# Attention bias loaded whole per head instead of formed on GpSimd, and gate rows summed one step later in the merge

## The chip, the cores and the metric

The kernel runs on one core of a Trainium2 chip. Its engines are TensorE (PE; its weight loads are listed apart as PEld), VectorE (DVE), ScalarE (ACT), GpSimd (POOL) and SyncE (SP), which here only issues DMA transfers; ACT and POOL issue some as well. Each engine works through its own instruction queue in order, and the engines meet through semaphores. The metric is the device time of one execution in microseconds, lower is better. Times are compared by the median of several executions.

## The reference, cut to what matters

One layer runs on 128 context tokens and 512 latent tokens (a grid of 8 rows by 64 columns) of width 1024. It has a Hyena branch and an attention branch on the same modulated input; they are gated, projected, merged and normalised. The change touches the bias of the neighbourhood attention and the gate of the merge:

```python
s_win = einsum("brqhd,brkhd->bhrqk", qg, kg) * scale
in_win = (key_col[None, :] >= c0[:, None]) & (key_col[None, :] < c0[:, None] + kw)
bias = rpb[:, dr + WIN_ROWS_MAX - 1, clip(dc + WIN_COLS - 1, 0, 2 * WIN_COLS - 2)]
s_win = where(in_win[None, None, None], s_win + bias[None], NEG_INF)
s_ctx = einsum("brqhd,bkhd->bhrqk", qg, ctx_k) * scale
p = softmax(concatenate([s_win, s_ctx], axis=-1), axis=-1)
...
p_h = (y_h * silu(g_h)) @ w_bh
p_a = (y_a * silu(g_a)) @ w_ba
out = (sigmoid(m_h) * p_h + sigmoid(m_a) * p_a) @ w_out
...
shift, scale, gate = split(silu(cond) @ w_ada + b_ada, 3)
x_new = layer_norm(ALPHA * x + gate * out)
```

There are 16 heads of width 64. The bias depends on the head and on the offset between query and key, the mask on the columns alone.

## The kernel before

**Precision.** Nearly every product is made of three passes of fp32r matmuls: both operands are split into a high and a low part. `split` (L100 to L102) makes the high part with a copy on ACT and the low part with a subtraction on DVE. A weight tile of 128 by 1024 is loaded into a `raw` buffer (two of them, `wraw`, L131), split into `wh` (two buffers) and `wl` (three buffers, `wtile`, L135) and used by 48 matmuls of 320 columns (`proj`, L173: 8 k-steps, 3 passes, 2 halves of the 640 tokens; one half to each of two PSUM banks). There are four PSUM banks of the kind `mm`, so two projections can be open at once.

**Order.** The program is traced in one order and then put in order for each engine by a planner that works with a simulated time. Only instructions in a `manual_schedule` block (the prologue on three engines; PE alone during attention) and those pinned by `keep_in_program_order` (behind the instruction traced before on the same engine) are placed by hand. `load_to` (L62) issues a load on SP and pins it while `pinned[0]` holds; that is so in the prologue and again from L1162, the merge, and not in attention.

**Attention (about 380 to 712 us).** For each pair of heads j = 0 to 7 there are four blocks b of 128 queries. `attention_setup` (L781) loads the mask, clears three strips of four `tm` tiles on POOL and forms the first two heads' tiles. `bias_tile` (L803) forms a head's bias tile `tm` (128 by 1024, negated, with the mask's fill): one load of 128 KB on SP into `tb` and three subtractions on POOL (L807, L810, L811), pinned from the third head on. `block_probs` (L878) asks for the next pair's two tiles at b = 1. `probs` (L826) adds tile and scores and takes the minimum in one DVE instruction (L833), then an exponential on ACT, a reciprocal on DVE and a scaling on POOL (L840). The queries are stored negated and scaled (`q_half`, L681), so the sum is the negated logit. `pair_tile` (L1012) runs beside this: it makes the projections for two weight tiles at a time from seven products, with sums of the tiles on DVE (L1023), splits (L101, L102) and evacuations on DVE (L1059, L1065).

**Merge (from about 712 us).** After attention, L1163 to L1168 load and split what is left of the Hyena branch's output `yh`; then a loop over n = 0 to 7 runs the projections `T_BH + n` (called BH0 to BH7 here) with the `yh` parts, and a second loop `T_BA + n` (BA0 to BA7) with the attention parts. Each turn of the first loop traces, in this order: the projection; the load of weight tile n + 2 (`wraw`); the load of `mh`; two gates on DVE that read the two PSUM banks (`gate`, L480, tile `mh`); the load of `yaraw`; its split into `ya_hH` and `ya_hL`; and one turn of `gate_rows` (L1176). A turn of `gate_rows` loads one row block of the gate's weights (512 KB, two buffers) and multiplies it into the two accumulators `gbc[:, 0]` and `gbc[:, 1]` on DVE (L1183 for the first, L1185 after). `out_weight` (L1190) loads and splits the output projection's tiles; for k below 4 into tiles `woh0` to `wol3` of the pool `lp`, first at the second turn of the BA loop.

Of the kernel before, what the change touches and what calls it, by code (L numbers as in the profile page):

```python
# [15 lines left out]
D = 1024  # L16
# [29 lines left out]
def tile_hyena_natten_step(ctx: ExitStack, tc: tile.TileContext, a, o):  # L46
# [634 lines left out]
    def q_half(j, hf, src):  # L681
        if f"q{j}" not in out:
            out[f"q{j}"], out[f"ql{j}"] = [slot(j, t, f"{t}{j}", F32R) for t in ("q", "ql")]
        q, ql = out[f"q{j}"], out[f"ql{j}"]
        parts = (
            ((slice(256, 576), slice(0, HALF)),) if hf else
            ((slice(0, 128), slice(0, 128)), (slice(128, 256), slice(192, 320)), (slice(576, NT), B7))
        )
        for cs, ss in parts:
            nc.scalar.activation(q[:, cs], src[:, ss], AF.Copy, scale=-0.125)  # L690
        for cs, ss in parts:
            nc.vector.scalar_tensor_tensor(ql[:, cs], src[:, ss], -0.125, f(q[:, cs]), op0=ALU.mult, op1=ALU.subtract)

# [84 lines left out]
    ac = ctx.enter_context(ExitStack())  # L778
    tms, edges, biases = [], {}, {}

    def attention_setup():  # L781
        nonlocal at, mask, sp, tp
        hy.close()
        sp = ac.enter_context(tc.tile_pool(name="sp", bufs=1, side="right"))
        tp = left.enter_context(tc.tile_pool(name="tp", bufs=1))
        at = ac.enter_context(tc.tile_pool(name="at", bufs=1, side="right"))
        mask = at.tile([P, 640], F32, tag="mask", name="mask")
        load_to(mask[:], a["mask"])
        for i in range(4):
            tm = at.tile([P, 1024], F32, tag=f"tm{i}", name=f"tm{i}")  # L790
            for c in (192, 448, 704):
                nc.gpsimd.memset(tm[:, c : c + P], 0.0)
            tms.append(tm)
        biases[0] = [bias_tile(h) for h in range(2)]
# [5 lines left out]

    at = mask = sp = tp = None

    def bias_tile(hd):  # L803
        tb = at.tile([P, 256], F32, tag="tb", bufs=2, name=f"tb{hd}")
        load_to(tb[:], a["rpbT"][hd])
        tm = tms[hd % 4]
        ins = nc.gpsimd.tensor_tensor(tm[:, :192], mask[:, :192], tb[:, 64:], op=ALU.subtract)  # L807
        if hd > 1:
            tc.keep_in_program_order(ins)
        nc.gpsimd.tensor_tensor(two(tm[:, 320:832])[:, :, :P], two(mask[:, 192:448]), two(tb[:]), op=ALU.subtract)  # L810
        nc.gpsimd.tensor_tensor(tm[:, 832:], mask[:, 448:], tb[:, :192], op=ALU.subtract)  # L811
        return tm
# [13 lines left out]
    def probs(j, b, s, tm):  # L826
        lo, hi = TWIN[b]
        res = []
        for h in range(2):
# [3 lines left out]
            ins = nc.vector.tensor_tensor_reduce(  # L833
                pv, s[h][:, : hi - lo], tm[h][:, lo:hi], 1.0, 3.0e38, ALU.add, ALU.min, accum_out=sm[:, 0:1]
            )
# [340 lines left out]
    def gate_rows():  # L1176
        for k in range(NK):
            raw = slot(k % 2, "v", f"gate{k}")[:, :D]
            load_to(raw, a["wgate"][k])
            for c in range(2):  # L1180
                s_ = st[:, k, c : c + 1]
                if k == 0:
                    nc.vector.tensor_scalar_mul(gbc[:, c], raw, s_)  # L1183
                else:
                    nc.vector.scalar_tensor_tensor(gbc[:, c], raw, s_, gbc[:, c], op0=ALU.mult, op1=ALU.add)  # L1185
# [28 lines left out]
    for n in range(NK):  # L1214
        ps = now(proj(T_BH + n, yhH, yhL))
        wraw(T_BH + n + 2)
# [110 lines left out]
def _host_constants():  # L1327
# [30 lines left out]
    for c in range(2):  # L1358
        sel[c::32, c] = 1.0
    mask = np.full((128, 640), BIG)  # L1360
    half, qc8 = np.arange(128) // 64, np.arange(128) % 8
    qc = half * 8 + qc8
    for m0, w, lo in ((0, 24, np.maximum(qc - 8, 0)), (192, 32, qc), (448, 24, 8 + np.minimum(qc - 8, 0))):
        j = np.arange(8 * w)
        key = (j // 64) * 8 + j % 8
        ok = (key[None] >= lo[:, None]) & (key[None] < lo[:, None] + 16)
        mask[:, m0 : m0 + 8 * w][ok] = 0.0
    c = dict(zemb=zemb, decay=decay, dft=dft.reshape(128, -1), sel=sel, mask=mask, ident=np.eye(128))
    return {n: np.ascontiguousarray(v, dtype=f32) for n, v in c.items()}
# [17 lines left out]
def _layout(inp):  # L1387
# [3 lines left out]
    def ktiles(w):  # L1391
# [16 lines left out]
    ci = np.clip((n // 64) * 8 + n % 8 - 8 - (p // 64) * 8 - p % 8 + 15, 0, 30)  # L1408
    rpbT = g["rpb"][0][:, ri, ci]
    ck = g["cache_k"][0, 0].reshape(128, 8, 128).transpose(1, 2, 0)  # L1410
    out = dict(
# [6 lines left out]
        fs1=np.stack([b1, fr[0]], axis=1), fs2=np.concatenate([fs2, fs2], axis=0),  # L1418
        rpbT=rpbT, ck=ck, cv=g["cache_v"][0, 0].reshape(128, 1024),
    )  # L1420
# [34 lines left out]
```

## Time and profile before

| what | value |
|---|---|
| executions timed | 898.63, 899.85, 900.48 us |
| median of the three | 899.85 us |
| time of the profiled execution | 900.47 us |
| span in its profile, first to last instruction | 898.5 us |
| mean granted TensorE clock | 0.993 |
| ACT busy | 423.4 us (47%) |
| bytes moved by DMA | 123.12 MB |
| of these on SP's and ACT's queues | 101.76 MB and 5.61 MB |

The profile is of one execution. It has a busy time for each engine, the share of the clock that the throttle granted to TensorE (PEclk), and for groups of instructions the engine's idle time just before them with what ended it. Matmuls overlap: each lasts some 310 ns and one starts about every 147 ns, so a busy PE says little and the number of matmuls started in a stretch says more. A count in a stretch includes those that were running when it began.

### The profile page before, as it was taken

What the parts mean: (1) busy time and instruction counts of PE and PEld (TensorE: products, weight loads), DVE (VectorE), ACT (ScalarE), POOL (GpSimd) and SP (SyncE); (2) the same over time, 40 slices, a digit from 0 to 9 for tenths busy, and PEclk for the clock granted to TensorE, in tenths of its full rate; (3) what the DMA queues carried; (4) which work ended last, traced back from release to release, by engine and by line L of the source; (5) the groups of instructions that cost most, each with busy time, mean ns of one, the idle gap of its engine ahead of it and who ended that gap; (6) DMA issues with size and microseconds to landing.
All of it is one profiled execution on the core that took longest, in us unless ns stands there. A gap on an engine that the chain in (4) does not pass through costs nothing. (4 is left out here: it accounts for less than half of the span.)

```text
span 898.5 us, 16909 instructions
## 1 busy us (share of the span) xinstructions
PE 880.2 (98%) x6560; PEld 850.8 (95%) x6560; DVE 625.6 (70%) x1229; ACT 423.4 (47%) x901; POOL 162.3 (18%) x188
## 2 busy tenths in 40 slices
PE   8999999999999999999999999999999999999994
PEld 7899999999999999999999999999999999999884
DVE  4776793794778568478977568756767568567565
ACT  4395455745445343355566455646655522233200
POOL 0010010101001000086654322332332000000000
PEclk9999999999999999999999999999999999999998
DMA  8975665665646223233243322332343577445332
GB/s 322 394 166 129 143 134 122 150 131 123 154 105 151 64 69 82 95 112 92 60 135 103 86 94 87 101 117 83 118 133 101 188 281 251 153 158 189 117 102 87
DMA packets 53835, 123.12 MB, mean 137 GB/s; under 512 B 8283, under 2 KB 25179, under 8 KB 53756
## 3 DMA queue, kind: packets, MB, share of 16 engines
q1 hardware_dynamic: 44108, 101.76, 35.2%
q0 software_dynamic: 4032, 14.68, 10.2%
q10 hardware_dynamic: 5616, 5.61, 1.8%
q8 instruction: 52, 0.85, 0.4%
q14 instruction: 27, 0.22, 0.1%
HBM read 107.87 MB, written 14.16 MB: 136 GB/s over the span
## 5 line engine op out<-in xcount | busy, mean ns | idle before, releaser
L168 PE MATMUL mm<-hH,wh 128*128 128x320 f32 x672 | 160.2, 312 | 1.8 <-ACT zs L471 1.0
L168 PE MATMUL mm<-hH,wl 128*128 128x320 f32 x672 | 158.5, 310 | 0.4 <-DVE wl L102 0.4
L168 PE MATMUL mm<-hL,wh 128*128 128x320 f32 x672 | 158.6, 311 | 0.0
L168 PEld LDWEIGHTS mm<-hH,wh 128*128 128x128 f32 x672 | 112.9, 188 | 4.7 <-issue 1.8
L168 PEld LDWEIGHTS mm<-hH,wl 128*128 128x128 f32 x672 | 113.5, 188 | 1.4 <-DVE wl L102 0.9
L168 PEld LDWEIGHTS mm<-hL,wh 128*128 128x128 f32 x672 | 113.3, 188 | 1.1 <-DVE hL L315 0.5
L1050 PE MATMUL sp<-t,wb 128*128 128x320 f32 x672 | 105.5, 310 | 0.0
L1050 PEld LDWEIGHTS sp<-t,wb 128*128 128x128 f32 x672 | 99.5, 188 | 0.3 <-issue 0.3
L1050 PE MATMUL sp<-hH,wb 128*128 128x320 f32 x336 | 81.9, 313 | 0.8 <-DVE c L1065 0.8
L101 ACT ACTIVATE wh<-raw 128x1024 fp32r<-128x1024 f32 x38 | 40.2, 1060 | 74.2 <-PE mm L168 41.9
L148 POOL DMA_DIRECT2D wl<-wall x28 | 24.4, 871 | 262.4 <-ACT wl L147 224.7
L102 DVE TENSOR_TENSOR wl<-raw,wh 128x1024 fp32r<-128x1024 f32 x38 | 47.4, 1250 | 25.8 <-ACT wh L101 25.4
L1050 PEld LDWEIGHTS sp<-hH,wb 128*128 128x128 f32 x336 | 57.9, 188 | 2.7 <-issue 2.7
L149 ACT ACTIVATE wh<-raw 128x1024 fp32r<-128x1024 f32 x28 | 29.7, 1061 | 52.7 <-PE mm L168 52.6
L102 DVE TENSOR_TENSOR wb<-s,wb 128x512 fp32r<-128x512 f32 x56 | 39.0, 701 | 19.7 <-ACT wb L101 19.5
L1050 PE MATMUL sp<-hL,wb 128*128 128x320 f32 x168 | 51.8, 309 | 0.0
L101 ACT ACTIVATE wb<-s 128x512 fp32r<-128x512 f32 x56 | 34.7, 628 | 34.8 <-DVE s L1023 21.0
L168 PE MATMUL mm<-yhs,wh 128*128 128x320 f32 x256 | 49.8, 315 | 1.0 <-DVE mh L481 1.0
L840 POOL TENSOR_SCALAR p<-p,sm 128x384 f32<-128x384 f32 x32 | 44.0, 1386 | 25.8 <-DVE sm L839 25.8
L1279 PE MATMUL out<-woh,yhs 128*128 128x512 f32 (+1 forms) x176 | 45.6, 373 | 0.0
L840 POOL TENSOR_SCALAR edge<-edge,sm 128x320 f32<-128x320 f32 x32 | 42.6, 1342 | 2.8 <-DVE sm L839 2.8
L168 PEld LDWEIGHTS mm<-yhs,wh 128*128 128x128 f32 x256 | 41.4, 193 | 1.2 <-ACT wh L101 1.2
(349 smaller groups left out, 2013.3 us busy)
## 6 DMA issues: line engine op xcount, KB each, us to landing
raw<-wall SPq DMA_DIRECT2D x96, 512.0 KB, 3.7
wl<-wall POOLq DMA_DIRECT2D x28, 512.0 KB, 5.7
ada<-wada SPq DMA_DIRECT2D x16, 512.0 KB, 8.1
gate<-wgate SPq DMA_DIRECT2D x8, 512.0 KB, 6.3
wo<-wall SPq DMA_DIRECT2D x8, 512.0 KB, 4.2
xt<-xT SPq DMA_DIRECT2D x8, 320.0 KB, 8.0
dec<-decay SPq DMA_DIRECT2D x20, 128.0 KB, 3.0
yh_d<-yh SPq DMA_DIRECT2D x8, 320.0 KB, 2.5
```

What stands on the lines that cost most here:

```text
L101: hi = nc.scalar.activation(dst_h, src, AF.Copy)
L102: return hi, (eng or nc.vector).tensor_tensor(dst_l, src, f(dst_h), op=ALU.subtract)
L148: nc.gpsimd.dma_start(wl, a["wall"][i], accum_op=ALU.add)
L149: nc.scalar.activation(wh, raw[:], AF.Copy)
L168: nc.tensor.matmul(ps[hf][:, :HALF], wt[k], x[:, hf * HALF : (hf + 1) * HALF], start=(i == 0 and k == 0), stop=(i == lead[2] and k == NK - ...
L840: nc.gpsimd.tensor_scalar_mul(pv, pv, sm[:, 2:3])
L1050: nc.tensor.matmul(dst, wk, x(xi, k), start=j < 4 and k == 0 and i == 0, stop=k == 3 and i == 2, skip_group_check=True,)
L1279: ins = nc.tensor.matmul(dst, m[k][:, c0 : c0 + P], w[:, c : c + n], start=(first and k == 0), stop=(last and k == 5), skip_group_check=True,)
```

## The change

The host lays out each head's bias tile whole: 128 by 1024 floats with the bias where the mask allows it, the large negative fill where it doesn't, and zeros in the strips of the context keys. Nothing is negated on the host; the latent queries are stored with scale +0.125 instead, and the sum in `probs` gets the factor -1.0. Context queries keep -0.125. `bias_tile` becomes one load of 512 KB into one of four `tm` buffers. The mask, the `tb` tiles, the clearing and the POOL subtractions go. In `gate_rows` the turn now ends between the load and the multiplications, so row block k is multiplied in at the next turn, and the first of its two multiplications is pinned behind the DVE instruction traced before it. BH2's split weights go to the tiles `woh0` and `wol0` of the pool `lp` instead of the `wh` and `wl` buffers.

```diff
-    def proj(i, xh=None, xl=None, eng=None):
+    def proj(i, xh=None, xl=None, eng=None, dst=None):
         if i in banks:
             return banks.pop(i)
-        w = wtile(i, eng)
+        w = wtile(i, eng, dst)
...
+        def scale(cs):
+            return -0.125 if cs.start == 0 else 0.125
+
         for cs, ss in parts:
-            nc.scalar.activation(q[:, cs], src[:, ss], AF.Copy, scale=-0.125)
+            nc.scalar.activation(q[:, cs], src[:, ss], AF.Copy, scale=scale(cs))
...
-        mask = at.tile([P, 640], F32, tag="mask", name="mask")
-        load_to(mask[:], a["mask"])
-        for i in range(4):
-            tm = at.tile([P, 1024], F32, tag=f"tm{i}", name=f"tm{i}")
-            for c in (192, 448, 704):
-                nc.gpsimd.memset(tm[:, c : c + P], 0.0)
-            tms.append(tm)
         biases[0] = [bias_tile(h) for h in range(2)]
...
     def bias_tile(hd):
-        tb = at.tile([P, 256], F32, tag="tb", bufs=2, name=f"tb{hd}")
-        load_to(tb[:], a["rpbT"][hd])
-        tm = tms[hd % 4]
-        ins = nc.gpsimd.tensor_tensor(tm[:, :192], mask[:, :192], tb[:, 64:], op=ALU.subtract)
-        if hd > 1:
-            tc.keep_in_program_order(ins)
-        nc.gpsimd.tensor_tensor(two(tm[:, 320:832])[:, :, :P], two(mask[:, 192:448]), two(tb[:]), op=ALU.subtract)
-        nc.gpsimd.tensor_tensor(tm[:, 832:], mask[:, 448:], tb[:, :192], op=ALU.subtract)
+        tm = at.tile([P, 1024], F32, tag="tm", bufs=4, name=f"tm{hd}")
+        load_to(tm[:], a["bias"][hd])
         return tm
...
             ins = nc.vector.tensor_tensor_reduce(
-                pv, s[h][:, : hi - lo], tm[h][:, lo:hi], 1.0, 3.0e38, ALU.add, ALU.min, accum_out=sm[:, 0:1]
+                pv, s[h][:, : hi - lo], tm[h][:, lo:hi], -1.0, 3.0e38, ALU.add, ALU.min, accum_out=sm[:, 0:1]
             )
...
             raw = slot(k % 2, "v", f"gate{k}")[:, :D]
             load_to(raw, a["wgate"][k])
+            yield
             for c in range(2):
                 s_ = st[:, k, c : c + 1]
                 if k == 0:
-                    nc.vector.tensor_scalar_mul(gbc[:, c], raw, s_)
+                    ins = nc.vector.tensor_scalar_mul(gbc[:, c], raw, s_)
                 else:
-                    nc.vector.scalar_tensor_tensor(gbc[:, c], raw, s_, gbc[:, c], op0=ALU.mult, op1=ALU.add)
-            yield
+                    ins = nc.vector.scalar_tensor_tensor(gbc[:, c], raw, s_, gbc[:, c], op0=ALU.mult, op1=ALU.add)
+                if c == 0:
+                    tc.keep_in_program_order(ins)
...
+    def wo_row(t, i, n):
+        return lp.tile([P, D], F32R, tag=f"{t}{i}", name=f"{t}{i}_{n}")[:]
...
-            wh, wl = (lp.tile([P, D], F32R, tag=f"{t}{k}", name=f"{t}{k}")[:] for t in ("woh", "wol"))
+            wh, wl = (wo_row(t, k, T_WO + k) for t in ("woh", "wol"))
...
-        ps = now(proj(T_BH + n, yhH, yhL))
+        ps = now(proj(T_BH + n, yhH, yhL, dst=[[wo_row(t, 0, T_BH + n)] for t in ("woh", "wol")] if n == 2 else None))
...
+    bias = np.zeros((16, 128, 1024))
+    for w, lo, r0, cols in (
+        (24, np.maximum(qc - 8, 0), 64, (slice(0, 192),)), (32, qc, 0, (slice(320, 448), slice(576, 704))),
+        (24, 8 + np.minimum(qc - 8, 0), 0, (slice(832, 1024),)),
+    ):
...
+        part = np.where(ok[None], rpbT[:, :, r0 : r0 + 8 * w], -BIG)
+        for cs, seg in zip(cols, np.split(part, len(cols), axis=2)):
+            bias[:, :, cs] = seg
```

More of the change, by code (lines that the diff above doesn't have):

```diff
@@ L778, in tile_hyena_natten_step @@
     ac = ctx.enter_context(ExitStack())
-    tms, edges, biases = [], {}, {}
+    edges, biases = {}, {}
     def attention_setup():
-        nonlocal at, mask, sp, tp
+        nonlocal at, sp, tp
         hy.close()
@@ L1359, in _host_constants @@
         sel[c::32, c] = 1.0
[L1360 to L1368, printed above, removed]
+    c = dict(zemb=zemb, decay=decay, dft=dft.reshape(128, -1), sel=sel, ident=np.eye(128))
     return {n: np.ascontiguousarray(v, dtype=f32) for n, v in c.items()}
@@ L1409, in _layout @@
     rpbT = g["rpb"][0][:, ri, ci]
+    half, qc8 = np.arange(128) // 64, np.arange(128) % 8
+    qc = half * 8 + qc8
+    bias = np.zeros((16, 128, 1024))
[3 more added lines that the diff above has]
+    ):
+        j = np.arange(8 * w)
+        key = (j // 64) * 8 + j % 8
+        ok = (key[None] >= lo[:, None]) & (key[None] < lo[:, None] + 16)
+        part = np.where(ok[None], rpbT[:, :, r0 : r0 + 8 * w], -BIG)
+        for cs, seg in zip(cols, np.split(part, len(cols), axis=2)):
+            bias[:, :, cs] = seg
+    bias = bias.astype(np.float32)
     ck = g["cache_k"][0, 0].reshape(128, 8, 128).transpose(1, 2, 0)
```

6 lines of the change are left out of this document (3 added, 3 removed).

## The prediction

> **What bounds the kernel now.** I read the page first, then PE's waits, then stretches of the span in which PE starts fewer matmuls than elsewhere, then the queues around the one such stretch that the change touches.
>
> ```profile
> span 898.5 us, 16909 instructions
> PE 880.2 (98%) x6560; PEld 850.8 (95%) x6560; DVE 625.6 (70%) x1229; ACT 423.4 (47%) x901; POOL 162.3 (18%) x188
> ```
>
> PE is the bound; no other engine comes near. So a change can only win time where PE stands still or is slow, and lose it by making PE wait. All the waits of PE that the trace shows:
>
> ```profile
> engine line waited for: us in total, times, longest us
> PE adaT L255 <- POOL spare L270: 1.5, 1, 1.5
> PE mm L168 <- ACT zs L471: 1.0, 1, 1.0
> PE mm L168 <- DVE wl L102: 1.0, 2, 0.6
> PE mm L168 <- DVE mh L481: 1.0, 1, 1.0
> PE sp L1050 <- DVE c L1065: 0.8, 1, 0.8
> ```
>
> Three things matter here. No wait names the bias tile or POOL's arithmetic. Attention has a single wait, 0.8 us (L1050). And the wait for `mh` and one for `wl` are in the merge. Stretches of the merge (start and end, then the busy time of PE, PEld, DVE, ACT and POOL with the number of instructions, the granted clock, the DMA share, GB/s):
>
> ```profile
> 712.70:726.75 14.05, 14.05 (x98) 14.04 (x96) 6.08 (x9) 4.76 (x7) 0.00 (x0) 1.00 0.78 258
> 726.75:737.45 10.70, 9.15 (x50) 8.63 (x49) 8.50 (x12) 3.04 (x5) 0.00 (x0) 0.84 0.84 297
> 737.45:744.50 7.05, 7.05 (x50) 7.05 (x49) 6.82 (x8) 1.81 (x3) 0.00 (x0) 1.00 0.61 214
> 729.75:733.17 3.42, 3.42 (x15) 3.42 (x14) 3.42 (x6) 0.00 (x0) 0.00 (x0) 0.50 0.74 239
> ```
>
> One projection, 50 matmuls counted, takes 7.05 us. The one from 726.75, BH2, takes 10.70: 3.65 us lost. Of these 3.42 x 0.5 = 1.71 are the clock at half, the other 1.94 are gaps. What made them, from the timeline (start, length, instruction, in brackets the idle time before and what ended it):
>
> ```profile
> 711.21 1.06 ACT L101 ACTIVATE wh<-raw 128x1024 fp32r<-128x1024 f32 x1 [0.45 <-PE sp L1050]
> 722.80 0.74 ACT L101 ACTIVATE ya_hH<-yaraw 128x640 fp32r<-128x640 f32 x1 [3.45 <-DMA yaraw<-ya_d]
> 726.16 2.15 ACT L101 ACTIVATE wh<-raw 128x1024 fp32r<-128x1024 f32 x2 [2.63 <-PE mm L168]
> 726.02 1.42 DVE L1183 TENSOR_SCALAR gbc<-gate,st 128x1024 f32<-128x1024 f32 x2 [1.63 <-DMA gate<-wgate]
> 727.35 0.88 DVE L481 SCALAR_TENSOR_TENSOR mh<-mh,mm 128x320 f32<-128x320 f32 x2
> 728.14 1.22 DVE L102 TENSOR_TENSOR wl<-raw,wh 128x1024 fp32r<-128x1024 f32 x1
> 726.55 0.46 PE L168 MATMUL mm<-yhs,wl 128*128 128x320 f32 x2
> 727.98 0.86 PE L168 MATMUL mm<-yhs,wh 128*128 128x320 f32 x4 [0.97 <-DVE mh L481]
> 729.42 0.64 PE L168 MATMUL mm<-yhs,wl 128*128 128x320 f32 x2 [0.58 <-DVE wl L102]
> ```
>
> BH2's weights could not be split before 726.16, because a `wh` buffer came free only then (BH1's split was at 711.21): 98 matmuls ran without a break from 712.70 to 726.75, so BH0 and BH1 are interleaved and end together, and both hold their `wh` to the end. At the same moment DVE was taken by the first gate row (726.02, 1.42 us), so the gate that empties BH0's banks began at 727.35 instead of about 726.3. PE waited for both, then for `wl`, and then ran at half clock.
>
> **The change part by part.** The sum is made against the profiled execution, 900.47 us; it stands 0.62 above the median of the runs, 899.85.
>
> *BH2 in its own tiles, gate row 0 later.* The raw tile of BH2 is not what was late: the wait at 726.16 ends on PE. With `woh0` and `wol0` free since attention's buffers closed, the split (1.06 on ACT, 1.22 on DVE) runs some time between 712 and 723, where ACT idles 3.45 us and more. Both waits for weights go. What is late next is the bank. BH0's last matmuls end about 0.15 us ahead of BH1's, at some 726.3. Between the start of the gate and PE's start in the rows above lie 727.98 - 727.35 = 0.63 us, so PE could go on at about 726.95, and its second matmul, which needs the second gate 0.44 later, at 727.4; without a wait it would start at 726.70 + 0.147 = 726.85 and then 727.0. That leaves about 0.3 us. If the second half of gate row 0, which isn't pinned, is put ahead of the gate as soon as its load lands (726.02), it takes 0.71 and PE starts at 726.02 + 0.71 + 0.63 = 727.36: about 0.7 in all. I take 0.5, between the two. The clock: two other gaps of PE show whether one gap alone lowers it.
>
> ```profile
> 240.00:242.00 2.00, 0.97 (x7) 0.78 (x6) 2.00 (x4) 2.00 (x7) 0.00 (x0) 1.00 0.51 104
> 570.00:572.00 2.00, 1.20 (x9) 0.97 (x8) 2.00 (x4) 1.35 (x6) 0.00 (x0) 1.00 0.00 0
> ```
>
> Gaps of 1.03 and 0.80 us left it at 1.00, so one of half a microsecond should. Term: -3.65 + 0.5 = -3.15, between -3.35 (0.3 left) and -1.25 (0.7 left and the clock's 1.71 again).
>
> [...]
>
> *The other gate rows.* Sixteen multiplications as before, each a turn later; the load of row k now waits for row k - 2, which stands behind the split of the next `yaraw`. Queued behind that load on SP are the next weight tile, `mh` and `yaraw`. The last row moves into BA0.
>
> ```profile
> L1185 DVE SCALAR_TENSOR_TENSOR gbc<-gate,st,gbc x14: 1277/1280/1286, 731.9 to 770.1; 128x1024 f32<-128x1024 f32 x14
> 728.84 0.74 ACT L101 ACTIVATE ya_hH<-yaraw 128x640 fp32r<-128x640 f32 x1 [0.53 <-DMA yaraw<-ya_d]
> 730.72 0.43 SPq L63 DMA_DIRECT2D gate<-wgate  x1
> 742.13 0.33 SPq L63 DMA_DIRECT2D raw<-wall  x1
> ```
>
> The third gate load went out at 730.72. Now it waits for row 0: split of `yaraw1` on ACT from 728.84 (0.74), its low part on DVE (smaller than a `wl`, so at most 1.22), then 1.42, so by 732.2 at the latest, 1.5 us late. But the weight tiles no longer wait on BH2's late split, and each projection gives 7.05 us to catch up. I cost it at 0; with no cover it would be one row pair, 2 x 1.28, once.
>
> *Attention on POOL.* Removed:
>
> ```profile
> L807 POOL TENSOR_TENSOR tm<-mask,tb x16: 588/605/1578, 384.2 to 632.2; 128x192 f32<-128x192 f32 x16
> L810 POOL TENSOR_TENSOR tm<-mask,tb x16: 733/743/1327, 384.8 to 602.7; 128x256 f32<-128x256 f32 x16
> L811 POOL TENSOR_TENSOR tm<-mask,tb x16: 594/602/1580, 385.5 to 604.5; 128x192 f32<-128x192 f32 x16
> L792 POOL MEMSET tm<- x12: 195/196/206, 380.1 to 381.7; 128x128 f32 x12
> ```
>
> 16 x (0.605 + 0.743 + 0.602) = 31 us at the medians and more with the long ones, and 12 x 0.196 = 2.4, all of it where PE doesn't wait: 0. The most that it could give is attention's one wait, 0.8, if DVE runs freer without POOL beside it. The scale's sign and the factor -1.0 leave every instruction in place: 0.
>
> *The loads.* 16 x 128 KB and the mask's 320 KB become 16 x 512 KB, about 6 MB more. The bus moved 408 GB/s at its best in the stretches that I read (726 to 728):
>
> ```profile
> 726.00:728.00 2.00, 1.03 (x8) 0.80 (x7) 1.98 (x4) 1.81 (x2) 0.00 (x0) 1.00 1.02 408
> raw<-wall SPq DMA_DIRECT2D x96, 512.0 KB, 3.7
> 380.25 0.41 SPq L63 DMA_DIRECT2D mask<-mask  x1
> 393.01 0.48 DVE L833 CUSTOM_DVE_ANT_0 edge<-s,tm 128x320 f32<-128x320 f32 x1
> ```
>
> So a tile takes 512 KB / 408 = 1.3 us of bus, a pair 2.6 where it took 0.65: 1.95 more for each pair. At the start four tiles may go out from 380.25: 4 x 1.3 and some 2.4 of latency (3.7 - 1.3) end near 388; the first use is at 393.01. Hidden. Later a pair's buffers come free with the last addition of the pair before, and from there I looked which weight load follows. The nearest of the six:
>
> ```profile
> 467.38 0.48 DVE L833 CUSTOM_DVE_ANT_0 edge<-s,tm 128x320 f32<-128x320 f32 x1
> 469.37 0.33 SPq L63 DMA_DIRECT2D raw<-wall  x1
> 473.14 0.69 DVE L1023 TENSOR_TENSOR s<-raw,raw 128x512 f32<-128x512 f32 x1 [1.82 <-DMA raw<-wall]
> 473.75 0.48 DVE L1065 TENSOR_TENSOR c<-sp,c 128x320 f32<-128x320 f32 x1
> ```
>
> Two bias tiles issued at 467.9 hold the bus to 467.9 + 2.4 + 2.6 = 472.9, and the weight tile lands 1.3 later, at 474.2, in place of 473.1: 1.1 us late, with DVE already waiting for it and an evacuation that PE needs queued behind. The planner may put the weight first, which costs nothing. I take +0.3, about a quarter of one such meeting; ends -0.8 (DVE freer) and +1.95 (one pair met in full).
>
> Sum: 900.47 - 3.15 + 0.3 = 897.6 for a profiled execution. If the 0.62 to the median carries over it is 897.0; if that gap is only the clock's 1.71 coming and going between executions, the median stays at 897.6. I take the middle, 897.3.
>
> **The rivals.**
>
> *Slower: the bias tiles stand ahead of weight tiles.* [...] DVE is first in line for the weights with no time in hand:
>
> ```profile
> DVE s L1023 <- DMA raw<-wall: 31.9, 13, 4.1
> ```
>
> Thirteen times it waited for a raw tile, 2.5 us each. If three of six pairs meet a weight load in full, 3 x 1.95 = 5.85 in place of 0.3: 902.9. It decides from two meetings on (3.9 against 3.15). For it: DVE's waits, and that the order on SP is planned anew. Against it: the six free times lie apart from the weight loads, but for the one shown. [...]
>
> *The merge's stall only changes its name.* If `mh`'s gate still comes late, because the pinned row or its unpinned half is planned ahead of it and waits for a load, the two gaps shrink little: 1.94 less a third, and the half clock stays. Back is then about 0.7: 900.47 - 0.7 + 0.3 less half of 0.62 = 899.8. For it: PE's first wait names `mh`. Against it: DVE idles 1.63 ahead of 726.02, so the gate needs only that nothing long is put before it.
>
> *The gap that is left lowers the clock.* 897.3 + 1.71 = 899.0. For it: at 726 gaps lowered it that singly did not elsewhere. Against it: the two rows with 1.00.
>
> *More is won.* The wait of 0.8 in attention goes too, and none is added: 897.3 - 0.3 - 0.8 = 896.2.
>
> **How the numbers follow.** Forecast 0.55, around 897.3 with its own range 896.4 to 898.3; slower by loads 0.17; stall renamed 0.12; clock 0.08; more won 0.08. What a measurement of this kernel can tell from no change is 0.2%, 1.8 us: below 898.05 is faster, above 901.65 slower. Faster: 0.55 less its upper 0.03, and 0.08, so 0.60. Same: 0.12 + 0.08 + 0.03, so 0.23. Slower: 0.17. The range reaches from 895.9 to 900.8: it takes in the stall renamed and one pair met, and leaves out most of the slower case.
>
> **What would show it.** The step in the merge is right if after the change the weights of BH2 are split before the BH0 and BH1 matmuls end, if PE's wait there is below 0.7 us, and if the clock stays at 1.00 up to the end; the stretch of one projection after BH1 is then near 7.5 us. It is wrong if PE still waits for `wl` or the clock shows 0.50 there. The step on POOL is right if its busy time falls by some 35 to 42 us and PE's time in attention doesn't follow. The step on the loads is wrong if PE waits in attention for `c` or `wb` by more than a microsecond in sum, with a bias load just ahead of a raw load on SP.

## The result, and the profile after

| what | before | after |
|---|---|---|
| median of 6 executions each, us | 900.16 | 896.14 |
| lowest to highest, us | 898.63 to 901.08 | 895.61 to 897.55 |
| ratio to before, with its 95% interval | | 0.9966 (0.9955 to 0.9978) |
| profiled execution, us | 900.47 | 897.23 |
| bytes moved by DMA, MB | 123.12 | 129.08 |

The forecast was 897.3 for the median and 897.6 for a profiled execution, and faster by over 0.2%. The change is faster by 0.34%, and the interval lies wholly below 0.998. The ratio comes from the comparison of the executions and isn't the quotient of the two medians, 0.9955.

From the page of the kernel after: its span, and busy time, share and instructions of each engine.

```profile
span 895.4 us, 16831 instructions
...
PE 878.3 (98%) x6560; PEld 849.8 (95%) x6560; DVE 619.9 (69%) x1229; ACT 423.0 (47%) x901; POOL 123.2 (14%) x128
```

POOL lost 39.1 us of its 162.3, DVE 5.7. The span is 3.2 shorter. Where this came from can be counted exactly, since PE starts the same 6560 matmuls in the same order: number them, and compare the start of the same matmul in both traces. The first 600 cost the changed kernel 0.40 us more (they take 64.7 to 65.9 us in the thirteen profiles of this case, whatever the kernel); then nothing changes for 500 us; between matmul 4300 and 4600, near 570 us, it wins 1.04; between 5500 and 5800, the start of the merge, 2.77; in the last stage 0.20; and after the last matmul it loses 0.43. That sums to 3.2 (898.54 - 895.37 = 3.17).

The same stretches of the merge as before, in the kernel after (start and end; busy time and instructions of PE, PEld, DVE, ACT and POOL; granted clock; DMA share; GB/s):

```profile
712.06:726.11 14.05, 14.05 (x98) 14.05 (x96) 6.83 (x9) 5.05 (x7) 0.00 (x0) 1.00 0.79 264
726.11:734.05 7.94, 7.34 (x50) 7.08 (x49) 6.95 (x10) 3.60 (x4) 0.00 (x0) 1.00 0.82 313
734.05:741.10 7.05, 7.05 (x50) 7.05 (x49) 6.22 (x8) 0.79 (x2) 0.00 (x0) 1.00 0.91 320
```

BH2 takes 7.94 us instead of 10.70, and the clock is at 1.00 throughout. 0.89 over the 7.05 of a projection without a wait is left. What is left shows in the timeline of the kernel after (start, length, instruction, in brackets the idle time before it and what ended that):

```profile
711.90 1.05 ACT L101 ACTIVATE woh<-raw 128x1024 fp32r<-128x1024 f32 x1
...
713.21 1.21 DVE L102 TENSOR_TENSOR wol<-raw,woh 128x1024 fp32r<-128x1024 f32 x1
...
725.77 0.75 DVE L1174 TENSOR_SCALAR gbc<-gate,st 128x1024 f32<-128x1024 f32 x1 [1.58 <-DMA gate<-wgate]
726.43 0.88 DVE L481 SCALAR_TENSOR_TENSOR mh<-mh,mm 128x320 f32<-128x320 f32 x2
...
726.97 0.56 PE L168 MATMUL mm<-yhs,woh 128*128 128x320 f32 x2 [0.60 <-DVE mh L481]
```

BH2's weights are split by 714.4, over 12 us ahead of their first use. The one thing that PE still waits for is `mh`'s gate, which stands behind the unpinned half of gate row 0; that half ran as soon as its load landed. And attention's wait is gone from the list of PE's waits (us in total, times, longest), which has no line for `sp` any more:

```profile
PE mm L168 <- ACT zs L471: 1.0, 1, 1.0
PE mm L168 <- DVE mh L481: 0.6, 1, 0.6
...
PE mm L168 <- DVE wl L102: 0.4, 1, 0.4
```

### The profile page after: what moved, and what is told of

Its sections match the earlier page's. It is cut to its first block, busy times and chain, and to the rows that moved or that the text cites. A ratio compares the mean times of both kernels' runs of the same rounds, so it can differ in the third digit from the quotient of the medians.

```text
span 895.4 us, 16831 instructions
## 1 busy us (share of the span) xinstructions
PE 878.3 (98%) x6560; PEld 849.8 (95%) x6560; DVE 619.9 (69%) x1229; ACT 423.0 (47%) x901; POOL 123.2 (14%) x128
## 2 busy tenths in 40 slices
DMA packets 53692, 129.08 MB, mean 144 GB/s; under 512 B 8268, under 2 KB 23116, under 8 KB 53613
## 5 line engine op out<-in xcount | busy, mean ns | idle before, releaser
L101 ACT ACTIVATE wh<-raw 128x1024 fp32r<-128x1024 f32 x37 | 39.1, 1059 | 78.6 <-PE mm L168 51.2
L102 DVE TENSOR_TENSOR wl<-raw,wh 128x1024 fp32r<-128x1024 f32 x37 | 45.4, 1229 | 26.7 <-ACT wh L101 26.0
L168 PE MATMUL mm<-yhs,wh 128*128 128x320 f32 x224 | 42.6, 309 | 0.0
L1274 PEld LDWEIGHTS out<-woh,yhs 128*128 128x128 f32 x176 | 32.0, 188 | 6.0
```

Of the source, the lines that this page charges most:

```text
L101: hi = nc.scalar.activation(dst_h, src, AF.Copy)
L102: return hi, (eng or nc.vector).tensor_tensor(dst_l, src, f(dst_h), op=ALU.subtract)
L168: nc.tensor.matmul(ps[hf][:, :HALF], wt[k], x[:, hf * HALF : (hf + 1) * HALF], start=(i == 0 and k == 0), stop=(i == lead[2] and k == NK - ...
L1274: ins = nc.tensor.matmul(dst, m[k][:, c0 : c0 + P], w[:, c : c + n], start=(first and k == 0), stop=(last and k == 5), skip_group_check=True,)
```

## The experiments

Eleven kernels ran, each beside the kernel before on the same chip. For each, worked out from its profile: the largest distance between two starts of matmuls near 570 us (0.27 where PE doesn't wait), the distances of the gaps behind BH1 (0.147 where there is none), whether the clock fell behind them, and the time from matmul 5500 to 5800, in which these gaps and the clock are all that differs.

```
kernel                 ratio to before (95%)     near 570   behind BH1    clock there  5500-5800
before, profile on which the prediction rests    1.11       1.28 + 0.88   0.50         47.62
after                  0.9966 (0.9955-0.9978)    0.27       0.91          1.00         44.85
e1 merge only          0.9977 (0.9964-0.9990)    0.69       0.92          1.00         44.88
e2 bias only           0.9998 (0.9984-1.0012)    0.36       1.15 + 0.88   1.00         45.95
e3 BH2 tiles only      0.9976 (0.9962-0.9989)    1.38       0.61          1.00         44.56
e4 gate rows only      0.9991 (0.9979-1.0004)    0.95       0.88 + 0.88   1.00         45.69
e5 after, again        0.9960 (0.9947-0.9974)    0.66       none          1.00         44.10
e6 both halves pinned  0.9963 (0.9949-0.9977)    0.27       none          1.00         44.11
e7 bias and tiles      0.9976 (0.9966-0.9987)    1.13       0.83          1.00         44.77
e8 POOL kept busy      0.9979 (0.9966-0.9992)    0.70       0.92          1.00         44.87
e9 before, again       1.0005 (0.9989-1.0020)    0.47       1.00 + 0.88   1.00         45.79
e10 wider bias tiles   0.9971 (0.9960-0.9983)    0.62       1.41          1.00         45.38
e11 fewer bias bytes   0.9960 (0.9944-0.9976)    0.27       none          1.00         44.12
```

**The merge's part alone.** The kernel before, with `gate_rows`, `wo_row` and BH2's `dst` of the change:

```diff
             load_to(raw, a["wgate"][k])
+            yield
...
-            yield
+                if c == 0:
+                    tc.keep_in_program_order(ins)
...
-        ps = now(proj(T_BH + n, yhH, yhL))
+        ps = now(proj(T_BH + n, yhH, yhL, dst=[[wo_row(t, 0, T_BH + n)] for t in ("woh", "wol")] if n == 2 else None))
```

> The kernel before with the merge's part of the change alone: gate rows a turn later, BH2's weights in their own tiles; the bias stays on POOL. Theory (the merge gives about three quarters, attention the rest): PE's gap behind BH1 shrinks to one of some 0.8 us and the clock stays at 1.00 there, 2.8 to 2.9 us are won in the merge, and attention's wait of about 1 us near 570 us stays: 2.8 below the kernel before, ratio 0.9969. Rival (the merge gives all of it, the attention difference is chance): the same 4.0 as the whole change shows in its medians, ratio 0.9956, and no wait near 570. Rival (the attention part gives most): below 1.5.

Measured 0.9977, 2.1 us where the theory had 2.8. The gap behind BH1 is 0.92 (some 0.8 was foreseen) and attention's wait is there (0.69 from start to start), so most of the gain is the merge's. The rival that the merge gives all of it is not excluded by the times: 0.9966 and 0.9977 have overlapping intervals.

**The bias alone.** The changed kernel with all of the diff above taken back: gate rows and BH2's buffers as before.

> The changed kernel with the merge's part taken back: bias tiles loaded whole, gate rows and BH2's buffers as before. Theory: the merge's stall of 3.65 us is back (two gaps and 3.4 us at half clock), and attention has no wait near 570 us: 1.0 below the kernel before, ratio 0.9989. Rival (bias loads cost as much as POOL's relief gives, the 1.0 was chance): 0, ratio 1.000, with the wait near 570 back. Rival (loads in the way): slower by 0.3 to 2.

Measured 0.9998: the times show no gain, and can't exclude one of 1.4 us (0.9984 to 1.0012). The profile shows no wait in attention. The unexpected thing is in the merge. Both gaps were back, 1.15 and 0.88, and the clock stayed at 1.00. So the two gaps by themselves don't lower it. The experiments on the clock, below, take this up.

**BH2's own tiles alone.**

```diff
-        ps = now(proj(T_BH + n, yhH, yhL))
+        ps = now(proj(T_BH + n, yhH, yhL, dst=[[wo_row(t, 0, T_BH + n)] for t in ("woh", "wol")] if n == 2 else None))
```

> The kernel before with BH2's own tiles alone; gate row 0 stays ahead of mh's gate on DVE. The gap before PE's first BH2 matmul stays (1.1 us lost), the second one, for wl, goes. Theory (a single gap of about a microsecond leaves the clock at 1.00): 3.65 - 1.13 = 2.5 below the kernel before, ratio 0.9972. Rival (this gap alone lowers the clock): 0.8 below, ratio 0.9991, with some 3.4 us at 0.50.

Measured 0.9976, as much as the whole part of the merge. The theory was right that one gap leaves the clock, but wrong about the gap: it was not 1.28 but 0.61, smaller than with the gate rows moved. The timeline of this kernel says why:

```profile
725.49 1.41 DVE L1183 TENSOR_SCALAR gbc<-gate,st 128x1024 f32<-128x1024 f32 x2 [0.99 <-DMA gate<-wgate]
726.82 1.78 DVE L481 SCALAR_TENSOR_TENSOR mh<-mh,mm 128x320 f32<-128x320 f32 x4
...
727.36 0.56 PE L168 MATMUL mm<-yhs,woh 128*128 128x320 f32 x2 [0.30 <-DVE mh L481]
```

The gate load landed at 725.49 here instead of 726.02, so both halves of row 0 were nearly done when BH0's bank was.

**The gate rows alone.** The two hunks of `gate_rows` from the merge's part, without `dst` and `wo_row`.

> The kernel before with the gate rows a turn later alone; BH2's weights still wait for the wh buffer that BH1 frees. The first gap shrinks to some 0.6 us, the wl gap stays near 0.7 (DVE makes wl behind the two gates). Theory (the clock falls when two gaps come close together): still 3.4 us at 0.50, 0.6 below the kernel before, ratio 0.9993. Rival (only the size counts, and 1.3 in sum is too little): the clock stays, 2.3 below, ratio 0.9974.

Measured 0.9991 (0.9979 to 1.0004). The first gap shrank only to 0.88, since one half of the row ran ahead here too; the second, for `wl`, stayed. The clock stayed at 1.00, so the theory fell. The rival's 0.9974 lies outside the interval: the gaps' sum fell only to 1.5, from 1.9 in the kernel before. In the stretch from 5500 to 5800 this kernel is 0.1 to 0.3 below the two others with both gaps and clock 1.00 (45.69 beside 45.95 for e2 and 45.79 for e9). In the profiles the move of the rows is worth little; the times (0.8 us, with an interval from a loss of 0.4 to a gain of 1.9) leave it open.

**The changed kernel again**, no edit.

> The changed kernel itself, beside the next three. In the profiles so far the clock falls only at whole multiples of 3.413 us from its first rise, and only behind a stretch in which PE stood still for half the time or more. Theory (the half clock in the merge of before is a matter of where this grid falls): no half clock behind BH1, since the one gap of 0.9 us can't fill half a stretch, and no wait near 570 us. Against the kernel before: 1.2 in the gaps, some 0.7 in the clock on average (1.71 in part of the executions), 0.8 to 1.0 in attention, 2.8 in all, ratio 0.9969. Rival (attention gives nothing on average): 1.9, ratio 0.9979.

Measured 0.9960 (0.9947 to 0.9974): the theory's 0.9969 lies inside the interval, the rival's 0.9979 outside. In its details the theory missed twice: this execution had no gap behind BH1 at all, and a wait near 570 us of 0.66. The 3.413 us of its grid are the length of the half clock in the first profile of before, from 729.753 to 733.166. Its premise, that the clock falls only behind stretches in which PE stood still for half the time, was too wide as well: e1's profile has a fall behind a stretch with PE busy for 3.21 of 3.41 us (last section). The half row that stood in the way in the first profile landed earlier:

```profile
724.31 0.76 DVE L1174 TENSOR_SCALAR gbc<-gate,st 128x1024 f32<-128x1024 f32 x1 [0.47 <-DMA gate<-wgate]
725.45 0.88 DVE L481 SCALAR_TENSOR_TENSOR mh<-mh,mm 128x320 f32<-128x320 f32 x2 [0.38 <-DMA raw<-wall]
```

So the gap that is left hangs on when one 512 KB load lands, 724.31 here and 725.77 in the first profile. That moves by more than a microsecond between executions of one kernel, and the wait near 570 us moves too, 0.66 from start to start here where the first profile has none (0.27).

**Both halves of the rows pinned.**

```diff
-                if c == 0:
-                    tc.keep_in_program_order(ins)
+                tc.keep_in_program_order(ins)
```

> The changed kernel with the second half of each gate row pinned as the first is, so that no part of row 0 stands ahead of mh's first gate. Theory: the gate starts as soon as BH0's bank is done, PE's gap behind BH1 falls from 0.9 us start to start to some 0.5, and 0.4 less than the changed kernel, ratio to the kernel before 0.9964. Rival (the gate is held up by the load of mh, not by the row): the gap stays at 0.9, ratio 0.9969.

The gap is gone: BH2's first matmul follows the last of BH1 at the usual distance, 0.147 us.

```profile
725.23 0.89 DVE L481 SCALAR_TENSOR_TENSOR mh<-mh,mm 128x320 f32<-128x320 f32 x2 [1.32 <-DMA raw<-wall]
...
725.78 0.56 PE L168 MATMUL mm<-yhs,woh 128*128 128x320 f32 x2
```

It gives what the changed kernel loses there where the load lands late, 44.85 - 44.11 = 0.74, and nothing where it lands early. The times (0.9963 beside 0.9960 and 0.9966) can't tell the two kernels apart.

**The bias and BH2's tiles, gate rows as before.** The changed kernel with the two hunks of `gate_rows` taken back.

> The changed kernel without the move of the gate rows: whole bias tiles, and BH2 in its own tiles. Theory (the move of the rows gives nothing; when BH2's split is early, row 0 lands early enough to be done before BH0 ends): PE's gap 0.6 to 0.9, the same as the changed kernel within 0.4, ratio 0.9966 to 0.9972. Rival (the row stands in the way, as in the kernel before): gap 1.3, 0.4 or more above the changed kernel, ratio 0.9974 or more.

Measured 0.9976, gap 0.83: the gap is the theory's, the ratio the rival's, 0.9 to 1.4 us above the changed kernel's two. In its profile the wait near 570 us (1.13) is larger than in any other kernel with whole tiles; whether its other executions have that wait too isn't known. So whether the moved rows give something on average stays open. They give nothing between e1 and e3.

**POOL kept busy.** Three subtractions of the old shapes per head, on a tile that nothing reads, two of them held to the additions that held the old ones (`extra` is set up once, and `sms` keeps the additions' results):

```diff
...
         load_to(tm[:], a["bias"][hd])
+        last = [sms.pop((hd - 4, b))[:, 0:1].to_broadcast([P, n]) if hd > 3 else extra[:, 512 : 512 + n] for b, n in ((2, 256), (3, 192))]
+        ins = nc.gpsimd.tensor_tensor(extra[:, :192], extra[:, 512:704], extra[:, 768:960], op=ALU.subtract)
+        if hd > 1:
+            tc.keep_in_program_order(ins)
+        nc.gpsimd.tensor_tensor(extra[:, 192:448], extra[:, 512:768], last[0], op=ALU.subtract)
+        nc.gpsimd.tensor_tensor(extra[:, :192], extra[:, 512:704], last[1], op=ALU.subtract)
...
```

> The changed kernel with three subtractions per head of the old shapes back on POOL, on a tile that nobody else uses, held to the same additions on DVE as the old ones were; the bias tiles are still loaded whole, and DVE's order is that of the changed kernel. Theory (POOL's work beside DVE lengthened DVE's instructions and with them the turn of the weight buffers): the kl pair near 555 us takes 1.0 instead of 0.48, and PE's wait near 570 us is back with 0.4 to 1.2 us; ratio 0.9976 to 0.9980. Rival (the wait went through the planner's order or the loads): no wait, DVE's lengths as in the changed kernel, ratio 0.9969.

The ratio is 0.9979, as the theory had it, 1.2 to 1.7 us above the changed kernel's two. PE's wait near 570 us is 0.70, but that alone shows little: with whole tiles and no subtractions on POOL it was 0.66 in e5 and 1.13 in e7. What tells them apart is the turn of the raw buffers: the time from the addition that waits for one pair of weight tiles to the issue of the next pair, on which PE's wait hangs. In the kernel before, the kernel after and this one:

```profile
551.66 0.69 DVE L1023 TENSOR_TENSOR s<-raw,raw 128x512 f32<-128x512 f32 x1 [2.50 <-DMA raw<-wall]
563.22 1.45 SPq L63 DMA_DIRECT2D raw<-wall  x2
...
552.10 0.69 DVE L1013 TENSOR_TENSOR s<-raw,raw 128x512 f32<-128x512 f32 x1 [2.75 <-DMA raw<-wall]
562.52 1.45 SPq L63 DMA_DIRECT2D raw<-wall  x2
...
552.63 0.69 DVE L1024 TENSOR_TENSOR s<-raw,raw 128x512 f32<-128x512 f32 x1 [3.13 <-DMA raw<-wall]
563.46 1.45 SPq L63 DMA_DIRECT2D raw<-wall  x2
```

The turn is 11.56, 10.42 and 10.83 us here. It is 11.5 in all five profiles with tiles formed on POOL and 10.4 in all five with whole tiles and no subtractions. In this kernel two of the subtractions fall into the turn before, near 539 us, which takes 8.7 us where all ten others take 7.9. So POOL's subtractions delay the weights, by 0.4 + 0.7 us here and by 1.1 in the kernel before. Of the 1.2 to 1.7 us in the ratios this profile shows PE's wait alone, some 0.4. Its execution took 896.76 us where the median of the kernel is 898.37, and where the others lose the rest isn't known.

The groups of DVE between 553 and 561 us (554 and 562 in the third) show how: line, operation, count, busy time, mean ns of one. First the kernel before, which has subtractions on POOL there:

```profile
L725 DVE TENSOR_TENSOR kl<-ck,k 128x128 fp32r<-128x128 f32 x2 | 1.0, 556 | 0.0
L1023 DVE TENSOR_TENSOR s<-raw,s 128x512 f32<-128x512 f32 x1 | 1.0, 987 | 0.0
L1065 DVE TENSOR_TENSOR c<-sp,u 128x320 f32<-128x320 f32 x2 | 0.9, 472 | 0.0
```

Then the kernel after, in which POOL does nothing until 558.68:

```profile
L1055 DVE TENSOR_TENSOR c<-sp,u 128x320 f32<-128x320 f32 x2 | 1.0, 476 | 0.0
L1013 DVE TENSOR_TENSOR s<-raw,s 128x512 f32<-128x512 f32 x1 | 0.7, 684 | 0.0
L728 DVE TENSOR_TENSOR kl<-ck,k 128x128 fp32r<-128x128 f32 x2 | 0.5, 282 | 0.0
```

And the kernel with POOL kept busy:

```profile
L1066 DVE TENSOR_TENSOR c<-sp,u 128x320 f32<-128x320 f32 x2 | 0.9, 474 | 0.0
L728 DVE TENSOR_TENSOR kl<-ck,k 128x128 fp32r<-128x128 f32 x2 | 0.9, 492 | 0.0
L1024 DVE TENSOR_TENSOR s<-raw,s 128x512 f32<-128x512 f32 x1 | 0.7, 682 | 0.0
```

`kl` takes 556 ns beside POOL, 282 without, 492 with POOL busy again; `s` 987 and 684, and 682 where the subtraction no longer fell on it (the planner put it elsewhere). In the kernel before, `wb` beside a subtraction takes 0.95 us at 558.91 and 0.67 in the kernel after. Together the three, with 0.55, 0.30 and 0.28, make the 1.13 by which the turn is longer. `c`, whose input `sp` comes from PSUM, is the same in all, 472, 476 and 474. By what means POOL's work lengthens the other three isn't shown.

**The kernel before again**, no edit.

> The kernel before, unchanged, against itself, for what two sets of executions of one kernel differ by and for the clock. The two gaps of the merge stand between PE's last BH1 matmul and 2.6 us later. Theory (grid): if one stretch of the 3.413 us grid that counts from the clock's first rise holds both gaps, the next stretch is at 0.50; if the grid cuts them, so that no stretch has 1.8 us of stillness, the clock stays at 1.00. Rival (the two gaps themselves lower the clock): 0.50 for some 3.4 us behind them wherever the grid lies. Ratio 1.000 within 0.0013.

The ratio 1.0005 with its interval tells what these comparisons can see: 0.15%. This execution had both gaps, 1.00 and 0.88, and the clock at 1.00. The clock first rose at 4.40 us here, at 6.13 in the first profile of the kernel before and at 5.25 in e2. Stretches of 3.413 us counted from there, the one with the gaps and the one that follows; first the kernel before:

```profile
726.34:729.75 3.41, 1.86 (x11) 1.33 (x10) 3.41 (x7) 2.68 (x3) 0.00 (x0) 1.00 0.79 317
729.75:733.17 3.42, 3.42 (x15) 3.42 (x14) 3.42 (x6) 0.00 (x0) 0.00 (x0) 0.50 0.74 239
```

The same for the kernel with the bias alone:

```profile
725.46:728.88 3.42, 2.01 (x12) 1.67 (x12) 3.42 (x7) 2.06 (x3) 0.00 (x0) 1.00 0.67 243
728.88:732.29 3.41, 3.41 (x25) 3.41 (x24) 3.41 (x4) 0.00 (x0) 0.00 (x0) 1.00 0.95 326
```

And for the kernel before, second profile:

```profile
728.02:731.44 3.42, 2.17 (x13) 1.90 (x14) 3.42 (x7) 1.90 (x3) 0.00 (x0) 1.00 0.76 258
731.44:734.85 3.41, 3.41 (x25) 3.41 (x25) 3.41 (x4) 0.00 (x0) 0.00 (x0) 1.00 0.93 334
```

In the first, both gaps fall into one stretch: PE was busy for 1.86 us of it and its weight loads for 1.33, and the next whole stretch is at 0.50. In the others the grid cuts a gap, 2.01 and 2.17 us are busy, and the clock stays. The theory fits all four profiles with both gaps, though only one of them has a fall. (In e4 too the grid cuts a gap, and PE is busy for 2.28 us of the stretch from 726.78.) The rival is out: e2, e4 and e9 have both gaps at 1.00.

**Wider bias tiles.**

```diff
-        tm = at.tile([P, 1024], F32, tag="tm", bufs=4, name=f"tm{hd}")
+        tm = at.tile([P, 1280], F32, tag="tm", bufs=4, name=f"tm{hd}")
...
-    bias = np.zeros((16, 128, 1024))
+    bias = np.zeros((16, 128, 1280))
```

> The changed kernel with bias tiles of 1280 columns in place of 1024 (the last 256 are zeros that nothing reads): 640 KB a head, 2 x 128 KB / 408 GB/s = 0.6 us more of the bus for each pair. Theory (the whole tiles give back part of what POOL's relief wins, by landing ahead of a weight tile): the weight tile that PE's wait near 570 us hangs on lands 6.7 us after its issue or later, where the profiles of whole tiles had 5.6 to 6.6 and those with tiles formed on POOL 5.4 to 6.0; the wait is 0.5 to 1.5 us; ratio 0.9967 to 0.9975. Rival (the bias loads are out of the weights' way): 5.4 to 6.0, a wait as in the changed kernel, ratio 0.9963.

**Only the columns in use.** With both halves of the rows pinned:

```diff
...
-        tm = at.tile([P, 1024], F32, tag="tm", bufs=4, name=f"tm{hd}")
-        load_to(tm[:], a["bias"][hd])
+        tm = tms[hd % 4]
+        load_to(tm[:, :192], a["bias"][hd][:, :192])
+        load_to(two(tm[:, 320:832])[:, :, :P], two(a["bias"][hd][:, 320:832])[:, :, :P])
+        load_to(tm[:, 832:], a["bias"][hd][:, 832:])
...
```

> The changed kernel with both halves of each gate row pinned, and with bias tiles of which only the 640 columns in use are loaded (three loads a head, 320 KB in all; the strips of zeros are cleared once on POOL), 2 x 192 KB / 408 GB/s = 0.9 us less of the bus for each pair. Theory (as above): the same weight tile lands 5.0 to 5.7 us after its issue, no wait near 570 us above 0.4, no gap behind BH1; 0.3 to 0.8 less than the changed kernel, ratio 0.9955 to 0.9960. Rival (bytes don't matter, or 32 more loads on SP cost as much): 0.9963 or more.

Counted from the issue of the first of the two weight loads to DVE's first use of both, the wider tiles gave 6.4 us and the smaller ones 5.8. In the kernel with wider tiles the issue of the pair and the addition that waits for it:

```profile
562.60 1.46 SPq L63 DMA_DIRECT2D raw<-wall  x2
...
569.00 0.69 DVE L1013 TENSOR_TENSOR s<-raw,raw 128x512 f32<-128x512 f32 x1 [3.09 <-DMA raw<-wall]
```

The same with the smaller tiles:

```profile
561.69 1.45 SPq L63 DMA_DIRECT2D raw<-wall  x2
...
567.45 0.69 DVE L1020 TENSOR_TENSOR s<-raw,raw 128x512 f32<-128x512 f32 x1 [2.29 <-DMA raw<-wall]
```

The theory's wait of 0.5 to 1.5 us was there with the wider tiles (0.62) and not with the smaller ones (0.27), but tiles of 512 KB have had both, and 6.4 misses its 6.7, and 5.8 its 5.7. The five profiles with tiles of 512 KB lie from 5.6 to 6.6 themselves (mean 6.1), the five with tiles formed on POOL from 5.4 to 6.0 (mean 5.6). So the whole tiles seem to delay the weight pair by about half a microsecond, and one profile for each size doesn't prove it. The ratio 0.9971 lies in the theory's range, but can't be put down to the loads: in that profile the half row started only at 726.71 and left a gap of 1.41 behind BH1. The kernel with the smaller tiles has neither gap nor wait; at 0.9960 it can't be told from the changed kernel.

## Why the prediction came out right

**BH2's tiles and gate row 0: right, with the clock mis-sized.** Foreseen were -3.65 + 0.5 = -3.15; the profile shows -2.77. The weights are split early, as foreseen, and both waits for them went. The gap that is left cost 0.89 and not 0.5: the unpinned half of the row did run ahead of `mh`'s gate, the end that was called 0.7. Of the 2.77, 1.06 are gaps and 1.71 the clock. That 1.71 belonged to the one profiled execution and not to the kernel. Of four profiles with both gaps (the first of before, e2, e4, e9) one shows the half clock. On average the gaps are worth 45.9 - 44.5 = 1.4 (45.9 for both gaps at full clock, 44.5 the mean of 44.85 and 44.10). A quarter of 1.71 would be 0.4 for the clock, but four profiles are few, and the record has the mean granted clock of every execution: 0.9943 on average in 94 of the kernel before and 0.9951 in 83 of the kernels whose BH2 has its own tiles. The 0.0008 are 0.7 us at full clock (0.4 to 1.0), an estimate, as they count falls anywhere in the span. So the step is worth some 2.1 on average, in place of 3.15. That the 1.71 might come and go between executions the prediction named in one sentence, and then took the whole of it into the term. Its rival that a gap left over lowers the clock is out: no gap of 0.6 to 1.4 us by itself did.

In the four profiles with both gaps the clock went with where the gaps fall in stretches of 3.413 us; the prediction had no such grid. The changes of the clock behind BH1 in the first profile of before, at 729.75 and 733.17, lie 212 and 213 such stretches behind its first rise at 6.13. The stretch with PE busy for 1.86 of 3.41 us was followed by half clock there, and those with 2.01, 2.17 and 2.28 (e2, e9, e4) weren't. What in a stretch decides isn't shown.

**The gate rows: cost 0, as forecast; a gain isn't shown.** The third gate load went out at 731.39 in the kernel after, 1.3 us later than before when counted from the last matmul of BH1 (at most 1.5 was foreseen), and PE did not wait for it. The gain was counted in with BH2's tiles. In the stretch from 5500 to 5800 the tiles alone give all of it: 44.56 and 44.77 with the rows as before (e3, e7), 44.85, 44.10, 44.87 and 44.88 with the rows moved (after, e5, e8, e1). Whether gate row 0 stood in the way hung on when its load landed: with one half still ahead of the gate there was no gap when that half started at 724.31 (e5) and one of 1.41 when it started at 726.71 (e10). With both halves pinned behind the gate (e6, e11) there was none. On the times e7 leaves the rows' worth open.

**POOL: the value 0 was wrong, its end -0.8 was the truth of the profile.** The cover that was named (PE doesn't wait for POOL) was right in the profile of before, and not the point. POOL's subtractions lengthened DVE's instructions (`kl` took 556 ns beside them and 282 without), and with them the turn of the two raw buffers: counted from the same matmul, the pair of weight loads ahead of the wait went out 1.1 us earlier in the five profiles with whole tiles than in the five with tiles formed on POOL, which is what DVE's instructions of the turn had been lengthened by (1.13 in the first profile of before). The wait, as the distance of two starts near 570 us, is 0.92 on average in the latter (1.11, 0.69, 1.38, 0.95, 0.47) and 0.54 in the former (0.27, 0.36, 0.66, 0.27, 1.13): 0.4 us, where the first pair of profiles showed 1.04. The two groups overlap, and so do the times from the weight pair's issue to DVE's first use (5.4 to 6.0 us and 5.6 to 6.6); so the earlier loads are shown, and the size of what PE gains by them is not. The rival "more is won" is what happened in the first pair: its 0.8 went, by the freer DVE that the term had named. The sign that was named for this step, that PE's time in attention wouldn't follow POOL's, failed.

**The bias loads: the meeting came, and cost PE nothing.** Near 570 us the tiles seem to delay the weight pair by half a microsecond (6.1 and 5.6 in the means of five profiles each); that this cost PE the 0.3 of the term isn't shown. At the place that the prediction named, near 468, the meeting did come, and PE lost nothing. The loads, an evacuation and the addition that needs the weight tile, in the kernel after:

```profile
469.01 0.86 SPq L63 DMA_DIRECT2D tm<-bias  x2
469.96 0.38 SPq L63 DMA_DIRECT2D raw<-wall  x1
...
471.92 0.49 DVE L1055 TENSOR_TENSOR c<-sp,c 128x320 f32<-128x320 f32 x1 [0.80 <-PE sp L1040]
475.78 0.69 DVE L1013 TENSOR_TENSOR s<-raw,raw 128x512 f32<-128x512 f32 x1 [2.36 <-DMA raw<-wall]
```

In the kernel before the addition started at 473.14, and PE's matmuls there are 0.40 earlier than in the kernel after: the tile came 2.2 us later, twice what was foreseen. But the evacuation, which stood behind the addition at 473.75, stands ahead of it now, at 471.92, and PE's starts from 460 to 490 us keep their distance of 0.40 within 2 ns. So what failed is the step from a late tile to a waiting PE. The row of the loads by kind (count, size, median us from issue to landing) has 4.6, where a weight tile takes 3.7:

```profile
raw<-wall SPq DMA_DIRECT2D x96, 512.0 KB, 3.7
...
tm<-bias SPq DMA_DIRECT2D x16, 512.0 KB, 4.6
```

The rival that the loads make the kernel slower is out.

**The sum.** 897.6 was forecast for a profiled execution and 897.23 came, by errors that cancel: the merge won 0.38 less than forecast, attention 1.34 more (1.04 won where 0.3 was to be lost), the last stage 0.20 more, 0.07 was won outside the spans, and 0.83 was lost in the prologue and behind the last matmul, which differ between any two executions. The median of 896.14 lies below the forecast's own range (896.4 to 898.3), at the 896.2 of "more is won"; the ratio 0.9966 on the 899.85 of before gives 896.8, which is inside. That the total came so near is in part luck. (The prediction's list of all of PE's waits has five of the nine in the trace; the four others, of 0.2 to 0.6 us, lie ahead of attention, and nothing rests on them.)

On average the parts that the record shows are 1.4 in the gaps, 0.7 in the clock, 0.4 in attention, 0.2 in the last stage and 0.2 outside the spans: 2.9 us. (An execution takes 1.97 us more than its span on average with tiles formed on POOL, 130 executions, and 1.80 with whole tiles, 71; why, isn't shown.) The ratios say 3.1 (2.0 to 4.1) and 3.6 (2.3 to 4.8), and both intervals hold 2.9. The 0.2 of the last stage come in four steps of some 0.05 in the output projection, in each kernel whose BH2 uses `woh0` and `wol0` and in neither e2 nor e4; their cause is open.

## What to carry to other kernels

A buffer that an interleaved pair holds to its end makes the third wait for both; a free buffer elsewhere ends that, here for some 1.2 us in the gaps and part of the clock's loss, without any added work. A clock loss in one profile is to be weighed with how often it happens before it goes into a sum: the same two gaps cost 47.6 - 44.1 = 3.5 us in one execution and 1.7 to 1.9 in two others. And an engine on which nobody waits can still cost time through the instructions that it slows on its neighbour (`kl` on DVE, 282 to 556 ns), so look at the same DVE group with and without POOL beside it.

## What was not expected of the hardware

**The grid of the clock.** Falls and rises after the first lie on whole multiples of 3.413 us from the first rise: in the first profile of before it came at 6.127 and the changes at 729.753, 733.166 and 890.179, 212, 213 and 259 multiples later; in the kernel after it came at 7.567 and the one fall at 888.206, 258 later. In e1 and e9 a fall came in the prologue, at 11.2 us. For e1 the stretch ahead of it and the one at half clock:

```profile
7.81:11.22 3.41, 3.21 (x19) 2.14 (x18) 2.08 (x5) 2.52 (x5) 0.00 (x0) 1.00 1.02 408
11.22:14.64 3.42, 3.38 (x13) 2.65 (x12) 3.38 (x5) 0.62 (x1) 0.00 (x0) 0.50 0.91 302
```

PE was busy for 3.21 us there by its records and the clock fell, so the busy share of the records is not what decides at this place, where other shapes of matmul run (in the first profile of before 128x256, 128x128, 128x2 and 33x320 between 7 and 11.6 us); what does was not tried. At the end of the kernel after it doesn't decide either: in the stretch from 881.38, in which the last matmuls run, PE is busy for 1.63 us and its weight loads for 1.42, and the next stretch is at 1.00. So the 1.86 behind BH1 is no threshold.

**The time of POOL's scalings.** In e9 the wait of PE for `p` in the first pair, for which the first profile of before has no line, cost 1.5 us:

```profile
PE pt L858 <- POOL p L840: 1.5, 1, 1.5
```

The two scalings of `edge` ahead of it took 4.85 us on POOL there and 4.12 in the first profile, the next two 3.74 and 2.76. Why they took longer was not tried. These scalings stand in the changed kernel too.
